# Cross entropy with label smoothing on one core: which engine waits for the last store

## The chip, the cores and the metric

The kernel runs on one core of one Trainium2 chip. A core has five engines with instruction streams of their own: PE (TensorE, matrix multiplication), DVE (VectorE), ACT (ScalarE), POOL (GpSimd) and SP (SyncE, which here issues transfers). [...] The metric is the device time of one execution in microseconds (us), the median over several runs.

## What is computed

There are 256 rows of 32000 logits, one label per row, and a smoothing of 0.1. For each row the result is the cross entropy against a target that spreads the smoothing evenly over all classes:

```python
log_probs = logits - np.max(logits, axis=-1, keepdims=True)
log_probs = log_probs - np.log(np.sum(np.exp(log_probs), axis=-1, keepdims=True))
smooth_targets = np.full((batch, num_classes), smoothing / num_classes)
for i, label in enumerate(labels):
    smooth_targets[i, label] = 1.0 - smoothing + smoothing / num_classes
return (-np.sum(smooth_targets * log_probs, axis=-1)).astype(np.float32)
```

Written out, the loss of a row is log(sum(exp(x))) minus a small weight times the sum of the row, minus a large weight times the logit at the label. So each row needs two sums over 32000 numbers and one gathered number. The input is 32.77 MB, the output one number per row, 1 KB in all.

## The kernel before

The 256 rows lie two to a partition over the 128 partitions. The first row of each partition is read in three pieces and the second in eleven, ever narrower ones (the table WIDTHS). Each piece is loaded by a transfer that SP issues (L284; the very first piece is shared between SP at L281 and ACT at L282). DVE sums a piece (L290) while ACT takes its exponentials and sums those (L305). POOL gathers the logits at the labels (L223) and finishes the first row.

After the last piece the second row is finished by a short chain over several engines: ACT takes the logarithm (L416), PE turns the column of 128 values into a row (L312, called from `row_of`), DVE adds the two parts into the tile `res` (L421), and SP issues the store of `res`, 1 KB, to memory (L429).

What follows the store is written out by hand. The framework would end a program with a barrier of all engines around the clearing of the semaphores that were used. The function `_end_one_by_one` (L63 to L149) takes the finished instruction lists of the program's last two blocks and rearranges them. In the trace all these instructions stand under L462, the line at which the program's context is closed. The order that it makes is this:

- In front of the store (L91 to L101), SP waits for everything except the store's own data, so that those waits are over when the data is there.
- After the store SP has a drain that waits for the data (L102 to L107).
- PE, ACT, DVE and POOL each have a drain, and each then adds one to a common semaphore (the `gather` semaphore; L118 to L132). After that they have no instruction left.
- SP waits until that semaphore is at 4 (L133), and then clears all semaphores that the program used, except the one on which the store reports that it has landed (`landed`; L88 and L134). The latter is number 118, the cleared ones are 99 to 117.
- The last instruction, `final` (L135 to L147), is an event instruction. It waits until semaphore 118 is at the value at which the store has landed (`store_wait`), and takes that value off again, so that the semaphore is at zero for the next execution.

Both functions that rearrange the program, this one and `_issue_first_transfers_at_start`, are run when it is finalized (L162 and L163). The instruction lists are per engine: an instruction's place is among those of its own engine, and moving one to another engine puts it at the end of that engine's list.

At the program's start there is a barrier too (L448 in the trace): the engines signal, POOL waits for them and releases them, and each has one event instruction that waits for this release.

Of the kernel before, what the change touches and what calls it, by code (L numbers as in the profile page):

```python
# [62 lines left out]
def _end_one_by_one(nc) -> None:  # L63

    body, end = nc.m.functions[0].blocks[1:]
    sync, pool = mybir.EngineType.SP, mybir.EngineType.Pool
    rest, closing = list(body.instructions), list(end.instructions)  # L70
    store = max(
        i for i, ins in enumerate(rest) if ins.engine == sync and ins.opcode == "DMACopy"
    )
    (landed,) = rest[store].sync_info.on_update
    data = {w.id for w in rest[store].sync_info.on_wait}
    first = closing[0]
    assert first.engine == sync and first.opcode == "Drain"
    waits = list(first.sync_info.on_wait)
    (store_wait,) = [w for w in waits if w.id == landed.id]
    clear = next(i for i, ins in enumerate(closing) if ins.opcode == "ISA")  # L80
    drain, cleared = closing[clear - 1 : clear + 1]
    assert cleared.engine == drain.engine == pool
    assert drain.opcode == "Drain" and drain.sync_info is None
    assert all(ins.opcode in ("Drain", "EventSemaphore") for ins in closing[clear + 1 :])
    fields, words = dict(cleared.ant_dict), list(cleared.instr)
    assert words[13:15] == [fields["range_first"], fields["range_last"]]
    assert landed.id == fields["range_last"] > fields["range_first"]
    fields["range_last"] = words[14] = landed.id - 1  # L88


    rest.insert(  # L91
        store,
        replace(
            drain,
            engine=sync,
            sync_info=mybir.SyncInfo(
                on_wait=[w for w in waits if w.id != landed.id and w.id not in data],
                on_update=[],
            ),
        ),  # L100
    )  # L101
    closing[0] = replace(  # L102
        first,
        sync_info=mybir.SyncInfo(
            on_wait=[w for w in waits if w.id in data and w.id != landed.id], on_update=[]
        ),
    )  # L107


    barrier = closing[1 : clear - 1]  # L110
    events = {sync: [], pool: []}
    for ins in barrier:
        if ins.engine in events and ins.opcode == "EventSemaphore":
            events[ins.engine].append(ins)
    gather, release = events[pool]
    (gathered,) = gather.sync_info.on_wait
    assert gathered.wait_value == 4
    drains = [ins for ins in barrier if ins.opcode == "Drain" and ins.engine != sync]  # L118
    assert len(drains) == 4
    for ins in drains:  # L120
        if ins.engine != pool:
            (signal,) = ins.sync_info.on_update
            assert signal.id == gathered.id and signal.update_value == 1
    final = next(
        ins for ins in closing[clear + 1 :]
        if ins.engine == sync and ins.opcode == "EventSemaphore"
    )
    closing[1:] = [
        *drains,
        replace(  # L130
            release, sync_info=mybir.SyncInfo(on_wait=[], on_update=[signal])
        ),  # L132
        replace(gather, engine=sync),  # L133
        replace(cleared, engine=sync, instr=words, ant_dict=fields),  # L134
        replace(  # L135
            final,
            sync_info=mybir.SyncInfo(
                on_wait=[store_wait],
                on_update=[
                    replace(  # L140
                        landed,
                        update_mode="sem-sub-imm",
                        update_value=store_wait.wait_value,
                    )
                ],
            ),
        ),  # L147
    ]
    body.instructions, end.instructions = rest, closing  # L149
# [3 lines left out]
def kernel(  # L153
# [7 lines left out]
    nc = tc.nc  # L161
    nc.at_finalize(_issue_first_transfers_at_start)  # L162
    nc.at_finalize(_end_one_by_one)  # L163
    B, C = logits.shape
    P = nc.NUM_PARTITIONS
# [301 lines left out]
```

The softmax here doesn't subtract the row's maximum and nothing guards it: scores larger than these inputs give would overflow.

## Time and profile before

| what | us |
|---|---|
| median of 6 runs | 82.9 |
| lowest and highest of them | 82.81, 83.07 |
| the profiled execution's own time | 82.86 |
| its span, first to last of the program's instructions | 81.53 |
| ACT busy | 57.8 |
| DVE busy | 37.0 |
| POOL busy | 10.0 |
| PE busy | 7.0 |
| the transfers' mean rate over the span | 402 GB/s |

The time is longer than the span: what an execution does before the program's first instruction and after its last is not in the span, but part of it is in the time.

In the views, an engine's name with a q (SPq, DVEq, PEldq) is its sequencer: the instructions that it handles by itself, such as waits on semaphores, drains and the issuing of transfers. They are not counted as busy. PE's instructions of that kind are shown under its weight-load half, PEldq. The view of a line lists all instructions recorded under it, those too. The view of waits gives who waited for whom: us in total, times, and the longest one. The chain that ended last is followed back from the last instruction that does work.

Beside the views the trace holds a list of the times at which each semaphore was updated, also before and after the program's own instructions. Times in it are in ns from the start of the span.

### The profile page before, as it was taken

The page shows a single profiled execution, that of the slowest core. Times are in us where ns is not written, and L with a number is a line of the kernel's source. Part 1 is how long each engine was busy: PE and PEld are TensorE (multiplying, and loading weights), DVE is VectorE, ACT ScalarE, POOL GpSimd, SP SyncE. Part 2 cuts the span into 40 slices and gives each one's busy share as a digit, 9 for nine tenths or more (in the row PEclk, how much of TensorE's full clock was granted, in tenths as well). Part 3 has the DMA queues.
Part 4 walks back from the last instruction along what each step waited for, and adds up shares of the span by engine and source line. Part 5 has one row for each costly group of instructions (what it writes and reads, how often), then busy time and mean ns, then how long its engine had stood idle before and what let it go on. Part 6 is the DMA issues. An engine that isn't in the chain of part 4 may idle for free.

```text
span 81.5 us, 215 instructions
## 1 busy us (share of the span) xinstructions
PE 7.0 (9%) x21; PEld 5.0 (6%) x21; DVE 37.0 (45%) x37; ACT 57.8 (71%) x31; POOL 10.0 (12%) x19
## 2 busy tenths in 40 slices
PE   0000000000000000000000000000100000399501
PEld 0000000000000000000000000000000000378300
DVE  0000001990000799400199801991097748467772
ACT  5000001999200799994199998999999999999991
POOL 3200640030100000000000001992000000000000
PEclk9999999999999999999999999999999999999999
DMA  6899999999999888998699899999999999999920
GB/s 132 368 480 401 455 566 392 392 392 392 514 612 411 362 362 362 588 497 362 269 539 438 370 522 394 414 414 402 425 425 401 433 419 441 417 413 412 412 79 1
DMA packets 2258, 32.77 MB, mean 402 GB/s; under 512 B 337, under 2 KB 338, under 8 KB 1106
## 3 DMA queue, kind: packets, MB, share of 16 engines
q1 hardware_dynamic: 2018, 30.71, 88.7%
q10 hardware_dynamic: 144, 2.06, 5.9%
q0 software_dynamic: 96, 0.00, 0.1%
HBM read 32.77 MB, written 0.00 MB: 402 GB/s over the span
## 4 chain that ended last, share of the span: by engine, by line
DMA 53%; ACT 44%; issue 1%; PE 0%; DVE 0%; ACTq 0%
DMA wide<-in_logits_dram 53%; ACT ja L305 25%; ACT jt L305 19%; PE lse_t L312 0%; DVE res L421 0%; ACT lse L416 0%; ACT lse L346 0%; ACTq L305 0%
## 5 line engine op out<-in xcount | busy, mean ns | idle before, releaser
L305 ACT ACTIVATE ja<-wide 128x8000 bf16<-128x8000 f32 (+4 forms) x5 | 40.2, 8033 | 21.0 <-DMA wide<-in_logits_dram 20.9
L290 DVE SCALAR_TENSOR_TENSOR jd<-wide 128x4000 f32<-128x4000 f32 (+11 forms) x12 | 34.5, 2876 | 39.0 <-DMA wide<-in_logits_dram 39.0
L305 ACT ACTIVATE jt<-wide 128x4608 bf16<-128x4608 f32 (+6 forms) x7 | 14.2, 2068 | 0.0
L407 PE MATMUL warm<-wide,ident 128*128 128x256 f32 x18 | 6.1, 510 | 11.7 <-DMA wide<-in_logits_dram 11.7
L407 PEld LDWEIGHTS warm<-wide,ident 128*128 128x128 f32 x18 | 4.7, 269 | 12.9 <-DMA wide<-in_logits_dram 12.0
L312 PE MATMUL loss_t<-ident,loss 128*1 128x128 f32 x1 | 0.4, 370 | 58.5 <-POOL loss L348 58.5
L337 POOL TENSOR_TENSOR lin<-acc,weighted 128x1 f32<-128x1 f32 x1 | 4.5, 4513 | 0.1
L312 PEld LDWEIGHTS loss_t<-ident,loss 128*1 128x1 f32 x1 | 0.1, 79 | 58.5 <-POOL loss L348 58.5
L332 POOL TENSOR_TENSOR acc<-sums 128x2 f32<-128x2 f32 x1 | 0.2, 192 | 16.1 <-ACT ja L305 16.1
L223 POOL DMA_INDIRECT gat<-in_logits_dram,flat_idx x2 | 2.0, 994 | 0.7 <-POOL ident masks.py:199 0.4
L351 DVE COPY res<-loss_t 1x128 f32<-1x128 f32 x1 | 0.3, 280 | 3.7 <-PE loss_t L312 3.7
L190 ACT ACT_TABLE_LOAD x1 | 1.3, 1283 | 0.9 <-PEq L448 0.9
L332 POOL TENSOR_TENSOR acc<-acc,sums 128x2 f32<-128x2 f32 x1 | 0.2, 193 | 12.6 <-ACT ja L305 12.6
L249 POOL TENSOR_SCALAR weighted<-gat 128x1 f32<-128x1 f32 x1 | 0.8, 761 | 6.5 <-DMA gat<-in_logits_dram,flat_idx 6.5
L305 ACT ACTIVATE jt<-tail 128x704 bf16<-128x704 f32 (+1 forms) x2 | 1.5, 766 | 0.0
L305 ACT ACTIVATION_READ_ACCUMULATOR jt<-wide 128x1 f32 x7 | 1.2, 171 | 0.0
L290 DVE SCALAR_TENSOR_TENSOR jd<-tail 128x352 f32<-128x352 f32 (+1 forms) x2 | 1.0, 508 | 0.0
L290 DVE DVE_READ_ACCUMULATOR jd<-wide 128x1 f32 x12 | 1.0, 81 | 0.0
L203 POOL DMA_DIRECT2D lab<-in_labels_dram x1 | 0.8, 766 | 1.0 <-POOLq L448 1.0
L305 ACT ACTIVATION_READ_ACCUMULATOR ja<-wide 128x1 f32 x5 | 0.9, 173 | 0.0
L215 POOL TENSOR_TENSOR flat_idx<-rowoff,lab 128x2 int32<-128x2 int32 x1 | 0.2, 193 | 5.3 <-DMA lab<-in_labels_dram 5.3
L249 POOL TENSOR_SCALAR xsum<-gat 128x1 f32<-128x1 f32 x1 | 0.2, 208 | 3.0 <-DMA gat<-in_logits_dram,flat_idx 3.0
(24 smaller groups left out, 4.7 us busy)
## 6 DMA issues: line engine op xcount, KB each, us to landing
wide<-in_logits_dram SPq DMA_DIRECT2D x1, 6240.0 KB, 25.9
wide<-in_logits_dram SPq DMA_DIRECT2D x1, 5760.0 KB, 39.1
wide<-in_logits_dram SPq DMA_DIRECT2D x1, 4288.0 KB, 29.6
wide<-in_logits_dram SPq DMA_DIRECT2D x1, 3200.0 KB, 20.5
wide<-in_logits_dram SPq DMA_DIRECT2D x1, 2304.0 KB, 25.5
wide<-in_logits_dram ACTq DMA_DIRECT2D x1, 2016.0 KB, 13.8
wide<-in_logits_dram SPq DMA_DIRECT2D x1, 1984.0 KB, 11.4
wide<-in_logits_dram SPq DMA_DIRECT2D x1, 1696.0 KB
```

The costliest lines, as they stand in the source:

```text
L190: nc.scalar.add_instruction(mybir.InstLoadActFuncSet(name=nc.get_next_instruction_name(), act_func_set_id=tbl, ins=[], outs=[],))
L203: nc.gpsimd.dma_start(out=lab[:], in_=labels.bitcast(I32).rearrange("(p f) -> p f", p=P))
L215: nc.gpsimd.tensor_tensor(out=flat_idx[:], in0=rowoff[:], in1=lab[:].rearrange("p (r two) -> p r two", two=2)[:, :, 0:1], op=ALU.add,)
L223: nc.gpsimd.indirect_dma_start(out=gat[:, r : r + 1], out_offset=None, in_=logits[:], in_offset=bass.IndirectOffsetOnAxis(ap=flat_idx[:, r ...
L249: nc.gpsimd.tensor_scalar(out=weighted[r], in0=gat[:, r : r + 1], scalar1=label_weight, scalar2=None, op0=ALU.mult,)
L290: return nc.vector.scalar_tensor_tensor(out=jd[:, :h], in0=xt[:, :h], scalar=1.0, in1=xt[:, h:w], op0=ALU.mult, op1=ALU.add, accum_out=out,)
L305: return nc.scalar.activation(out=ja[:, :w], in_=xt[:, :w], func=AF.Exp, accum_out=out)
L312: nc.tensor.transpose(out=row[:], in_=column, identity=ident[:])
L332: nc.gpsimd.tensor_tensor(out=acc[:], in0=total, in1=sums[:, :, t : t + 1], op=ALU.add)
L337: nc.gpsimd.tensor_tensor(out=lin[:], in0=total[:, 0, :], in1=weighted[0], op=ALU.add)
L351: nc.vector.tensor_copy(out=res[:, :, 0:1], in_=loss_t[:])
L407: nc.tensor.matmul(warm[:], lhsT=ident[:], rhs=xt[:, i * WARM_COLS : (i + 1) * WARM_COLS], start=True, stop=True,)
```

## The change

The last instruction, `final`, is given another engine. The framework made it as one of SP's; the changed line makes it one of PE's. What it waits for and what it does to semaphore 118 stay as they are. On PE it stands behind PE's drain. SP's list now ends with the clearing of the semaphores 99 to 117. Nothing else in the program differs.

```diff
@@ -134,6 +134,7 @@
         replace(cleared, engine=sync, instr=words, ant_dict=fields),
         replace(
             final,
+            engine=mybir.EngineType.PE,
             sync_info=mybir.SyncInfo(
                 on_wait=[store_wait],
                 on_update=[
```

## The prediction

> **What bounds the kernel now.** I read the page's chain first, then the chain in order of time near the end, the groups of the program's closing line L462 and of its opening line L448, SP's own waits, and last a list that no view prints: the times at which semaphores were updated.
>
> The page's part 4, the chain that ended last, by engine:
>
> ```profile
> DMA 53%; ACT 44%; issue 1%; PE 0%; DVE 0%; ACTq 0%
> ```
>
> The span is loads and then exponentials; nothing that the change touches is in it. The chain in order of time shows what leads to the store (start us, us, what):
>
> ```profile
> 79.77 0.28 PE lse_t L312
> 80.05 0.02 issue
> 80.08 0.28 DVE res L421
> ```
>
> and the timeline shows the store that SP issues next:
>
> ```profile
> 80.38 0.32 SPq L429 DMA_DIRECT2D out_dram<-res  x1
> ```
>
> So from 80.36 us on there is only the store and the closing. The reader is to see that the edit can act only on the stretch from here to the end of the timed execution. What runs there is in the groups of L462, where the whole epilogue is recorded (instruction, durations in ns min/median/max, first and last start us):
>
> ```profile
> L462 SPq EVENT_SEMAPHORE  x7: 17/28/28, 74.5 to 81.5; - x7
> ...
> L462 ACTq DRAIN  x1: 291/291/291, 79.5 to 79.5; - x1
> L462 PEldq DRAIN  x1: 323/323/323, 79.8 to 79.8; - x1
> L462 DVEq DRAIN  x1: 306/306/306, 80.1 to 80.1; - x1
> L462 SPq EVENT_SEMAPHORE_RANGE_CLEAR  x1: 58/58/58, 81.0 to 81.0; - x1
> ```
>
> and SP's own waits say what it still waited for:
>
> ```profile
> SPq L429 <- DVE res L421: 1.7, 1, 1.7
> ...
> SPq L462 <- SPq L462: 0.4, 1, 0.4
> ```
>
> The last row is the wait in question: SP's range clear runs from 81.045 to 81.103 us, the store's semaphore (118) gets its last increment at 81.500, and SP's last instruction runs from 81.517 to 81.534, where the span ends. The clear is 0.4 us early; the landing of the store sets the end, on either engine. PE has had nothing to do since its drain ended at 80.086.
>
> The last rows that matter are those of the start-up barrier, L448, because PE there executes the kind of instruction that is to move:
>
> ```profile
> L448 SPq EVENT_SEMAPHORE  x1: 17/17/17, 0.8 to 0.8; - x1
> L448 ACTq EVENT_SEMAPHORE  x1: 17/17/17, 0.8 to 0.8; - x1
> L448 DVEq EVENT_SEMAPHORE  x1: 21/21/21, 0.8 to 0.8; - x1
> L448 PEldq EVENT_SEMAPHORE  x1: 51/51/51, 0.8 to 0.8; - x1
> ```
>
> **After the program's last instruction.** The profiled execution took 82.86 us, its span 81.53: 1.33 us lie around it. The list of semaphore updates shows what runs after it. Semaphore 2, which the program does not use, is updated nine times in each of two rounds (ns from the span's start):
>
> ```
> first round   80331  80365  80404  80604  81665 | 81710  81748  81782  81829
> second round  82615  82650  82688  82741  82765 | 82866  82905  82939  82985
> ```
>
> Between them, from 81.78 to 82.39 us, nearly all other semaphores are written once, in five blocks of consecutive numbers. The same round of nine stands before the program, from -0.375 to -0.005 us, when nobody is late.
>
> I read a round as a line of five engines, up and back down, each update released by the one before. The first comes 245 ns after PE's drain ended (80.086), although POOL had signalled its end at 58.85 and ACT's drain had ended at 79.75. The second and third follow 34 and 39 ns apart: ACT and POOL, long done. The fourth comes 203 ns after DVE's drain ended (80.401), the fifth 131 ns after SP's last instruction. So the order is PE, ACT, POOL, DVE, SP and back, PE being released last. SP stands at the turn, PE at the outermost place. SP arriving late costs half a round after it, PE arriving late costs a whole one.
>
> **The change part by part.** One instruction goes from SP's stream to PE's, and nothing is issued or transferred anew.
>
> Removed from SP: one event instruction of 17 ns. SP then arrives 131 ns after its clear, at 81.234, which is hidden by the store's landing at 81.500. Were that cover gone (a store landing before 81.1), SP would be the late one and this would still not save anything on PE's path.
>
> Added to PE: it stands behind PE's drain, which ended 1.4 us before the landing; no program instruction is queued behind it. Who waits for it is the whole round. In four terms, against this execution:
>
> 1. Waking. SP started 17 ns after the landing. At the start-up release (update at 0.809 us) SP started after 16 ns, PE after 28. I take 28: start at 81.528, +11.
> 2. Executing. 51 ns on PE for 17 on SP: end at 81.579, +34. Here the span ends, so it grows from 81.53 to 81.58.
> 3. From the instruction's end to the engine's update of semaphore 2: 131 ns on SP; on PE 245, measured behind a drain. The trace of before has no PE event at this place. Below it is bounded by SP's 131, above by 315, the time from PE's release before the program (-0.005) to its first drain (0.310). I take 245, the same engine at the same place. PE's update is at 81.824, where SP's was at 81.665: +114 for this term, +159 so far.
> 4. The round. With SP late, its last update came 164 ns after SP's (81.665 to 81.829). With PE first and nobody else late it takes 370, in the second round (82.615 to 82.985) and in the one before the program alike. +206: PE is released at 82.194 instead of 81.829.
>
> Sum: +365 ns. What follows is released engine by engine from this round, PE's release being the last; the block that is written last (numbers 3 to 53, 82.04 to 82.39) begins 0.2 us after it, and the others are finished by 82.18. The second round cannot begin before that block is done, so it moves by the whole sum. SP's earlier arrival gives nothing back, since it too is released later (81.968 for 81.665).
>
> The bounds: with terms 1 to 3 at SP's prices only term 4 is left, +206; with 315 in term 3 it is +435. The profiled execution, 82.86, would become 83.22; the median of the runs shown is 82.9, 0.04 above it, which gives 83.26.
>
> [...]
>
> **Rivals.** (a) PE is as quick as SP here. The 245 may hold what a drain leaves behind and a plain event does not. For it: SP's 131 is behind an event, DVE's 203 and PE's 245 are behind drains. Against it: PE's 51 ns row. Only the round remains: +0.21, 83.11.
>
> (b) No measurable change. The time might not take in the two rounds in the way I think, or the added part might lie beside other closing work; then only the span's growth of 0.045 shows: 82.95. Against it: the second round ends 1.45 us after the span, near the 1.33 that the time adds, so both rounds seem to be inside.
>
> (c) Faster: the order is one of arrival, and whoever arrives last is released first. Then PE, whose block is the slowest, starts it before the others: terms 1 to 3 cost up to 159, and the 164 ns that PE waited behind SP, DVE, POOL and ACT are saved. At PE's prices that is level, at SP's it is -0.16, 82.74; it decides for faster only if PE's terms 1 to 3 come to less than 164, by more than what can be measured only if they come to nothing. For it: SP arrived last and its successors follow in 45 ns. Against it: the rounds in which nobody is late have the same gaps (35, 38, then 44 or 53, 23) as the one in which ACT and POOL had been done for long, and their updates waited for PE's.
>
> (d) Dearer: a PE that has waited on a semaphore for 1.4 us resumes more slowly than the start-up row shows, another 0.1 to 0.2 us: 83.4. No row speaks for it.
>
> **How the numbers follow.** The sum as worked out has 0.72, (a) 0.16, (b) 0.05, (c) 0.04, (d) 0.03. The likeliest is 83.26. Its bounds, 82.9 plus 0.206 and 0.435, are 83.11 and 83.34; the runs of before spread from 82.81 to 83.07, so a median may be off by some 0.04, which gives 83.07 to 83.38. That holds the sum and (a), and leaves (b), (c) and (d) out. About 0.2% (0.17 us) is what a measurement of this kernel can tell from no change: 83.07 is just the edge. The sum and (d) are over it and (a) mostly is, so slower has 0.89; same has 0.07 from (b) and the low edge of (a), faster 0.04 from (c).
>
> **What would show it.** Right: the profile after has its span at 81.58 with a PE event of about 51 ns as the last instruction, SP's clear still near 81.05 to 81.10; the first round of semaphore 2 begins only after the landing, about 0.3 us later, and then runs through its nine updates in about 370 ns; the time outside the span grows from 1.33 to about 1.65. Step 3 is wrong if the first update stands nearer to 130 than to 245 ns behind PE's event. Step 4 is wrong if the round's first updates still come at 80.33 to 80.60, or if PE's is not the first. The forecast as a whole is wrong if the time outside the span does not move, or if the store's landing itself moves by tenths of a us, which nothing in the edit explains.

## The result and the profile after

The changed kernel takes 83.26 us (median of 23 runs, 83.11 to 83.44); the kernel before takes 82.91 us (49 runs, 82.69 to 83.27). The ratio is 1.0037, with a 95% interval from 1.0029 to 1.0046: slower by 0.24 to 0.38 us by the ratio, 0.35 by the two medians.

The page looks as it did, with the same shares in the chain that ended last:

```profile
DMA 53%; ACT 44%; issue 1%; PE 0%; DVE 0%; ACTq 0%
```

The groups of the closing line, which is L463 now (durations in ns min/median/max, then first and last start in us), show the edit itself:

```profile
L463 SPq EVENT_SEMAPHORE  x6: 17/28/28, 74.7 to 81.2; - x6
...
L463 ACTq DRAIN  x1: 292/292/292, 79.6 to 79.6; - x1
L463 PEldq DRAIN  x1: 323/323/323, 79.9 to 79.9; - x1
L463 DVEq DRAIN  x1: 308/308/308, 80.3 to 80.3; - x1
L463 SPq EVENT_SEMAPHORE_RANGE_CLEAR  x1: 58/58/58, 81.2 to 81.2; - x1
L463 PEldq EVENT_SEMAPHORE  x1: 51/51/51, 81.7 to 81.7; - x1
```

SP has six event instructions where it had seven, and its last instruction is the clear. PE has one of 51 ns, and with it the span ends. Accordingly SP's last wait, the row with 0.4 us, is gone from its waits:

```profile
SPq L430 <- DVE res L422: 1.7, 1, 1.7
SPq L463 <- DMA tail<-in_logits_dram: 0.7, 1, 0.7
```

The profiled execution took 83.41 us with a span of 81.76: 1.65 us lie around it, where there were 1.33. But its span is also 0.23 longer, five times the 0.046 that the slower event adds (29 and 51 ns to start and run on PE, for 17 and 17 on SP). The timeline says why; this is the store:

```profile
80.56 0.32 SPq L430 DMA_DIRECT2D out_dram<-res  x1
```

It was issued 0.18 us later than in the profile before, ahead of anything that the edit touches. That is scatter between executions: in a second profile of the unchanged kernel (below) the store is issued later still, at 80.67. So two profiles are best compared from the store's landing on, the last increment that the store makes to semaphore 118. These are the nine updates of semaphore 2 in the first closing round, in ns from the landing:

```
before   -1169  -1135  -1096   -896    165 |  210   248   282   329
after      320    355    393    436    460 |  557   596   630   677
```

Before, four updates had been made long ago and five were left. After, none has been made when the store lands: PE's, the first, comes at 320, and the whole round of 357 ns follows. The round ends 348 ns later than before. The second round ends 1855 ns after the landing instead of 1485, +370; in another profile of the changed kernel it is 1833, +348.

What the time counts can be read off too: in twelve of the thirteen profiles of this study the time is the end of the second round less 0.118 to 0.134 us (the thirteenth, with DVE waiting twice, is told below), whichever engine was late. So what delayed the closing rounds lengthened the time by as much in these twelve.

### The profile page after: what moved, and what is told of

The parts are those of the page before. It is cut to its first block, busy times and chain, and to the rows that moved or that the text cites. A ratio compares the mean times of both kernels' runs of the same rounds, so it can differ in the third digit from the quotient of the medians.

```text
span 81.8 us, 215 instructions
## 1 busy us (share of the span) xinstructions
PE 7.5 (9%) x21; PEld 5.3 (6%) x21; DVE 37.0 (45%) x37; ACT 57.8 (71%) x31; POOL 10.1 (12%) x19
## 4 chain that ended last, share of the span: by engine, by line
DMA 53%; ACT 44%; issue 1%; PE 0%; DVE 0%; ACTq 0%
DMA wide<-in_logits_dram 53%; ACT ja L306 24%; ACT jt L306 19%; PE lse_t L313 0%; DVE res L422 0%; ACT lse L417 0%; ACT lse L347 0%; ACTq L306 0%
## 5 line engine op out<-in xcount | busy, mean ns | idle before, releaser
L408 PE MATMUL warm<-wide,ident 128*128 128x256 f32 x18 | 6.6, 548 | 11.7 <-DMA wide<-in_logits_dram 11.7
```

The lines of the kernel that those rows point to most:

```text
L408: nc.tensor.matmul(warm[:], lhsT=ident[:], rhs=xt[:, i * WARM_COLS : (i + 1) * WARM_COLS], start=True, stop=True,)
```

## The experiments

The theory was that two things add up: the place of the waiting engine in the closing round (what is left of the round after it) and the price of that engine's own instructions. The rival was the price alone, with 164 ns of round after whichever engine is late.

### The same wait on each engine

The edit is the one of the change, with another engine each time:

```diff
         replace(
             final,
-            engine=mybir.EngineType.PE,
+            engine=mybir.EngineType.Activation,
```

and in the same way Pool and DVE; PE was run once more beside them.

> The changed kernel once more, as the fourth of a row with the other engines on one chip. Place and price (my theory: the closing round of semaphore 2 runs PE, ACT, POOL, DVE, SP and back, and the late engine pays its own slowness and what is left of the round after it): from the store's landing to the first round's last update about 677 ns as in the first profile of the changed kernel, 320 of it up to PE's own update and 357 of round; 83.26 us. Price alone (rival: the round costs the same 164 ns after whoever is late, and PE is just a slow engine): the same total, but then the round after PE's update would have to be 164, which the first profile does not show. Both expect some 0.35 us over the kernel before.

> The store's last wait on ACT. Place and price: ACT woke after 21 ns and took 17 ns at the start-up release; its way to its own update lies between SP's 131 and PE's 240, I take 150, so ACT updates semaphore 2 some 190 ns after the landing (170 to 280). PE's update, the first of the round, comes early, at about 80.3; after ACT's some 325 ns of round are left (357 to 370 less 35). Landing to the round's end about 515 ns, against 329 on SP: +0.19, 83.10 us. Price alone: 190 + 164 = 354, +0.02, 82.93 us, no change that can be measured.

> The store's last wait on POOL. Place and price: waking about 17 and executing 17 ns, then 131 to 240 to its update, 150 taken: 185 after the landing. PE's and ACT's updates come early; some 290 ns of round are left (357 to 370 less 35 and 38). Landing to the round's end about 475 ns: +0.15, 83.06 us. Price alone: 185 + 164 = 349, +0.02, 82.93 us.

> The store's last wait on DVE. Place and price: waking 27 and executing 21 ns, then 203 ns as behind its drain before: 251 after the landing. PE, ACT and POOL update early; about 245 ns of round are left, among them the slow step of about 100 ns from SP back to DVE, which is 45 when DVE has long been waiting. Landing to the round's end about 495 ns: +0.17, 83.08 us. Price alone: 251 + 164 = 415, +0.09, 83.00 us. Over the four engines place and price expects the rest of the round to shrink from PE over ACT and POOL to DVE: 357, 325, 290, 245, with 164 on SP.

Measured, with ns from the store's landing (SP's row is the profile before; its time is the one measured beside these four). The rest of the round runs from the late engine's own update to the round's last:

| waits for the store | event starts, takes | that engine's update | rest of the round | first round ends | time, us | ratio to before, interval |
|---|---|---|---|---|---|---|
| SP | 17, 17 | 165 | 164 | 329 | 82.90 | |
| DVE | 27, 21 | 238 | 241 | 479 | 83.17 | 1.0037 (1.0021 to 1.0053) |
| POOL | 24, 17 | 626 | 285 | 911 | 83.60 | 1.0074 (1.0055 to 1.0093) |
| ACT | 22, 17 | 188 | 322 | 510 | 83.15 | 1.0035 (1.0016 to 1.0053) |
| PE | 28, 51 | 320 | 357 | 677 | 83.35 | 1.0055 (1.0036 to 1.0073) |

The moved event as the groups of the closing line show it, with ACT and with DVE waiting:

```profile
L463 ACTq EVENT_SEMAPHORE  x1: 17/17/17, 81.5 to 81.5; - x1
L463 DVEq EVENT_SEMAPHORE  x1: 21/21/21, 81.5 to 81.5; - x1
```

For PE, ACT, POOL, DVE and SP the rest of the round is 357, 322, 285, 241 and 164, against 357, 325, 290, 245 and 164 expected; PE's and SP's were known from the profiles before and after, the other three were forecasts. Price alone, which expects 164 for all, is refuted. The updates also show the order directly, since the long gap always stands in front of the late engine's own update (ns from the landing):

```
PE late       320    354    392    436    460 |  557   596   630   677
ACT late    -1183    188    226    269    293 |  389   429   463   510
POOL late   -1168  -1134    626    670    694 |  791   830   864   911
DVE late    -1179  -1145  -1107    238    262 |  359   398   433   479
SP late     -1169  -1135  -1096   -896    165 |  210   248   282   329
```

The gap moves from the first place to the fifth: PE, ACT, POOL, DVE, SP.

Two prices were missed. POOL needs 585 ns from its event's end (24 + 17) to its update; 131 to 240 had been expected. The event itself is quick, as the groups of the closing line of that kernel show:

```profile
L463 POOLq EVENT_SEMAPHORE  x2: 17/17/17, 59.0 to 81.7; - x2
```

And with DVE waiting the time is 0.1 us above what the first round gives. In its profile DVE's update in the second round comes 190 ns after POOL's, where it is 43 to 54 in all the other profiles. DVE was held up once more, later; by what, the runs do not show.

### Scatter, and an event on PE that is not late

The kernel before was run once more, unchanged, and beside it one in which PE has an event more, but early. It stands in front of PE's drain and waits for a value that semaphore 118 had long before:

```diff
     closing[1:] = [
+        replace(
+            final,
+            name=nc.get_next_instruction_name(),
+            engine=mybir.EngineType.PE,
+            sync_info=mybir.SyncInfo(
+                on_wait=[replace(store_wait, wait_value=store_wait.wait_value // 2)],
+                on_update=[],
+            ),
+        ),
         *drains,
```

> The kernel before once more, unchanged, for a second profile of it: how much the pieces after the store's landing differ between executions of one program. Both theories: 17 + 17 + 131 ns from the landing to SP's update and 164 ns of round, each within some 20 ns; 82.9 us.

> SP waits for the store as before. PE gets one event instruction more, ahead of its drain, that waits for a value the semaphore has had since 67.6 us. Place and price: PE reaches the round about 0.1 us later than before, near 80.4 us, and over 1 us ahead of SP, so nothing moves: 82.9 us, landing to the round's end 329 ns. Rival (an event instruction on PE costs by being there, through PE's instruction stream or the size of its program): +0.05 to +0.13, and a later round.

The unchanged kernel: landing to SP's update 165, to the end of the round 329, to the end of the second 1482 ns, in two profiles the same within 3 ns. Its time came out at 83.06 us (12 runs) beside 82.87 for itself, ratio 1.0020 (0.9999 to 1.0040). So a median of this size may be off by 0.2 us, while the pieces after the landing repeat to a few ns: where hundredths count here, the semaphore updates decide, not the medians.

The early event is there in the groups, ahead of the drain:

```profile
L471 PEldq EVENT_SEMAPHORE  x1: 51/51/51, 79.8 to 79.8; - x1
L471 PEldq DRAIN  x1: 310/310/310, 80.0 to 80.0; - x1
```

and costs nothing: PE's update comes 1176 ns before the landing, the round ends 328 ns after it, the time is 82.95 us against 82.87, ratio 1.0007 (0.9994 to 1.0020). An event of 51 ns on PE did not cost by being there; late, as in the changed kernel, it went with a round that ended 348 ns later.

### One event more on each engine

What is the way from an engine's last event to its update made of? The waiting engine waits twice, and only the second event changes the semaphore. On SP:

```diff
+        replace(
+            final,
+            name=nc.get_next_instruction_name(),
+            sync_info=mybir.SyncInfo(on_wait=[store_wait], on_update=[]),
+        ),
         replace(
             final,
```

On the other engines both events also have that engine's name in an `engine=` line.

> SP waits for the store twice, with two event instructions one behind the other; the second changes the semaphore. This prices one sequencer instruction on SP at the very end: 55 ns from the end of one event to the next instruction (as between SP's earlier event and its clear) and 17 ns of its own: landing to the round's end 329 + 72 = 401 ns, +0.07, 82.98 us.

> PE waits for the store twice in the same way. If PE's 240 ns from its event to its update are the price of PE's sequencer for the same few instructions that take SP 131 (my reading of the third term), one more instruction costs on PE about 72 x 240 / 131 = 130 ns: 51 of its own and some 80 ahead of it; landing to the round's end 677 + 130 = 807 ns, 83.39 us. If the 240 holds something that happens once (a fetch of what comes after the program, a flush of PE's queue), the second event costs no more than its 51 ns and SP's gap of 55: 106 or less, 83.36 us or less.

> ACT waits for the store twice, two events in a row. The question is what the way from an engine's last event to its update of semaphore 2 is made of: 131 ns on SP, 149 on ACT, 190 on DVE, 241 on PE and 585 on POOL, while one more event cost 57 on SP and 110 on PE. Theory (a few sequencer instructions after the program, each at the engine's own price): the tail is about 131/57 = 2.3 such prices everywhere, so one more event on ACT costs 149/2.3 = 65 ns, and ACT's update comes 188 + 65 = 253 ns after the landing. Rival (the tail is a thing of its own): one more event costs ACT what it cost SP, 53 to 57: 243. The two lie close together here; DVE and POOL tell more.

> DVE waits for the store twice. Theory: 190/2.3 = 83 ns more, DVE's update 238 + 83 = 321 ns after the landing, then 241 of round. Rival: SP's gap of 36 and DVE's own 21, 57 ns: 295.

> POOL waits for the store twice. POOL's 585 ns from its event to its update were not expected. If its sequencer is that slow per instruction: 585/2.3 = 254 ns more, the update at 626 + 254 = 880 ns after the landing. If something at the end of POOL's program happens once (it stood hidden before, since POOL was done 22 us ahead of the others): about 53 to 65 as on SP and ACT, the update near 685, and 285 of round after it.

| engine | last event's end to update, ns | one event more moves the update by | quotient of the two |
|---|---|---|---|
| SP | 131 | 58 | 2.3 |
| ACT | 149 | 54 | 2.8 |
| DVE | 190 | 75 | 2.5 |
| PE | 241 | 109 | 2.2 |
| POOL | 585 | 60 | 9.8 |

PE's two events are the same 51 ns each:

```profile
L469 PEldq EVENT_SEMAPHORE  x2: 51/51/51, 81.7 to 81.9; - x2
```

with 60 ns between them (79 to 139 ns after the landing), where SP's take 17 with 36 between. PE paid about twice what SP paid for one such instruction, 109 ns to 58, and its way to the round was longer by nearly the same factor, 241 to 131. On SP, ACT, DVE and PE the quotients, 2.2 to 2.8, fit loosely with a few instructions at each engine's own price, but this is argued, not shown, for the runs do not tell the two readings apart: SP's 58 came where 72 was expected; PE's 109 lies between the 130 of the one reading and the 106 of the other, and scaled from 58 instead of 72 the 130 would be 106 as well; ACT's 54 is what the rival expected (53 to 57, where the theory had 65); DVE's 75 is nearer the theory's 83 than the rival's 57.

On POOL the second event is as cheap as on SP (60 and 58 ns), so its 585 ns are not explained by a higher price of every instruction. If POOL's way were made like SP's, it would be an estimated 140 ns (2.3 times 60), and some 450 would be a thing of its own behind the program's last instruction; what that is, no run shows. In the kernel before, POOL had been done for 22 us, and its way to the round was hidden.

Median times of the two that were timed: SP twice 83.05 us, ratio 1.0021 (1.0007 to 1.0036), not to be told from the unchanged kernel's 83.06; PE twice 83.37, ratio 1.0053 (1.0039 to 1.0067). A single execution of each of the others took 83.09 (ACT), 83.38 (DVE) and 83.55 us (POOL). DVE's is again higher than its rounds explain: the second round less 0.125 us would give 83.03. In its profile the block of semaphores 156 to 206 starts 429 ns after the first round's end, where it is 15 to 17 in all the others. The second round is not later for it, so what made the time 0.35 us longer is not seen in the rounds, and whether it is the same hold-up as with one event on DVE is not shown.

## Why the prediction was right

The time, 83.26, is the one forecast, in part by luck: the scatter of a median is larger than the agreement, and the same kernel took 83.35 beside the other engines. The terms can be checked one by one.

- **What bounds the end.** The store's landing ends SP's wait before and PE's after. SP's clear ended 0.40 us ahead of the landing in both, so SP's being free sooner gave nothing, as said.
- **Term 1, waking.** 29 and 28 ns in the two profiles for the 28 taken from the start-up barrier.
- **Term 2, executing.** 51 ns for 51. The row of the start-up barrier could be carried over unchanged.
- **Term 3, event to update.** 240 and 241 for 245, measured behind a drain. Rival (a), a PE as quick as SP behind a plain event, is refuted by this number alone.
- **Term 4, the round.** 357 for 370. Against the second round of the kernel before, POOL to DVE took 43 instead of 53 and the step behind SP's update 97 instead of 101; against the round ahead of the program only that last step is much shorter, 97 instead of 111. So +193 instead of +206.
- **The sum.** +348 at the end of the first round for the +365 of the working.
- **What follows.** That the second round moves by the whole sum holds: from the end of the first round to the start of the second it was 786 ns before and 786 in the second profile of the changed kernel. In the first it was 818, and this, with a second round shorter by 10, makes its +370. The link that was assumed shows too: in all thirteen profiles the second round's first update comes 224 or 225 ns after the last write into the block 3 to 53, while the time between the rounds varies from 781 to 818.
- **Rival (b), no measurable change,** is refuted by the time outside the span, 1.65 for a forecast of about 1.65, and by the tie between the time and the end of the second round.
- **Rival (c), the last to arrive is released first,** is refuted by the rounds with each engine late: the order stays PE, ACT, POOL, DVE, SP, and the block 3 to 53 begins 214 to 248 ns after the round's end whichever engine was late, PE too.
- **Rival (d), a slower waking after a long wait,** is refuted by the 29 ns after 1.4 us of waiting.

Two sentences of the prediction were off. It expected a span of 81.58, and the profile has 81.76; it also said that a landing moved by tenths of a us would count against the forecast. Neither tells anything: the unchanged kernel scatters by as much (81.53 and 81.83), before the store is issued. SP's later release was put at 81.968; the steps of the two rounds used give 81.964 or 81.974, and nothing rests on it.

## What to carry to other kernels

When a step waits for the very last event of a kernel, the engine that executes it can matter after the program has ended: in these runs a late engine pays its own way to the closing round and all of the round that is still ahead of it. Here SP, at the turn of the round, is the cheapest of the five places, with 164 ns of round left after its update, and PE the dearest by place, with 357; the same wait costs 329 ns to the end of the first round on SP, 479 on DVE, 510 on ACT, 677 on PE and 911 on POOL. An event that PE executed early cost nothing: the round ended 328 ns after the landing, for 329 without it. So it is worth trying small closing work on engines that are done early, and the last wait on the one with the shortest way out; such differences are read from the semaphore updates after a common event, not from spans.

## What was not expected

POOL takes 585 ns from its last event to its update, where one event more costs only 60; what the rest is was not tried. With DVE as the last, something later is held up once more (a step of 190 ns for some 50 in one profile, the block 156 to 206 some 0.4 us late in another); this stays open. And the stretch from the store's landing to the end of the first round repeats to 1 ns over three profiles in which SP waits once (329, 329, 328), while the store's issue moves by 0.29 us among them.
